# Merged input in half-length tiles, and FFN operands two blocks wide made in steps between the quarters of the projection

## The chip, the cores and the metric

The kernel runs on one core of one Trainium2 chip. The metric is the device time of one execution in microseconds (us), from which medians over executions are taken. The core's engines are TensorE (PE, with its weight loads as PEld), VectorE (DVE), ScalarE (ACT), GpSimd (POOL) and SyncE (SP, which here only issues transfers).

## The reference, cut to what matters

It is one layer of an encoder on 64 sample tokens and 1024 prompt tokens (T = 1088) of width 1024: token mixing in two branches, a gated merge, an output projection with a residual add, and a SwiGLU feed-forward network (FFN) with a hidden width of 2816, then a last norm. The part from the merge on is, in the notation of the reference:

```
m  = gate_a * (ya @ w_a) + gate_b * (yb @ w_b)          # merge
x1 = x + g1 * (m @ w_out)                               # output projection, residual
u  = rmsnorm(x1, norm2_g) * (1 + scale2) + shift2       # FFN input
h  = silu(u @ w_ff_gate) * (u @ w_ff_up)                # 1024 -> 2816
y  = rmsnorm(x1 + g2 * (h @ w_ff_down), final_g)        # 2816 -> 1024
```

Everything is float32. Before and after the change each float32 product is made of three matmuls: an operand is split into a high part (a cast to a format of fewer bits, "hi") and the remainder ("lo", a subtraction), and hi·hi, hi·lo and lo·hi are added up.

## The kernel before, in words

Activations lie transposed, 128 channels on the partitions and tokens along the free dimension, in eight channel blocks (KB = 8). The tokens are worked in two halves of HT = 544, each of two quarters of QT = 272. The stages that matter here follow each other as below; the times of the stages are in the next section.

**Merge** (L978 to L994). `mh` and `ml` are the merged input, split, in 16 tiles of all 1088 tokens in the pool `mp`.

**Output projection.** `wo_half(m, h, ws)` (L1051) makes channel block m of token half h by two calls of `wo_quarter`; each quarter is 24 matmuls (8 input blocks by 3), an add of the residual on DVE (L1040) and a square on ACT (L1046, tile `sq`). POOL adds the squares of m up to 5 into `acc`. The weights of the first half are split on POOL (`w_unit`: L52 makes hi, L58 lo), as are those of the second half, which are loaded again.

**Norm of a half.** `rstd_rows(h, sqs)` (L1077) adds the squares over the channels by matmuls against a column of ones (`ps_ss`, L1087: three sources, `acc` and the last two `sq`, for six token cuts, so 18), turns them into 1/sqrt on DVE and ACT (`v` L1090 and L1093, `rs` and `r` L82 to L87), spreads the result over the partitions by six matmuls (`ps_rr`, L1099) and copies it (L1102).

**FFN operands.** Gate and up are a Strassen-Winograd product of seven partial products, in the order 1, 6, 5, 7, 2, 3, 4. For a token half h the operand of product p is `ops[h, p]`, tiles `b{p}h` and `b{p}l`. `modulate2(h, j, r)` makes those of 1, 6, 5 and 7 from the pair of channel blocks j and j + 4: a multiplication by the norm (L1119, 128x1088), the modulation on ACT (L1123), three differences of 128x272 (L1128, L1129, L1132), an update (L1134) and four splits. `modulate2_rest(h, j)` splits those of 2, 3 and 4. For h = 0, modulate2 is called after every second m of the second half of the projection, and modulate2_rest after the last; for h = 1 both are called once after each of the first four jobs below. In all there are four calls of each for a half.

**Gate and up** (L1235 to L1306). The list `jobs` goes over the 22 blocks of 128 hidden channels: the first NF = 8 for the first token half alone, then 14 blocks for both halves, then the first 8 for the second half ("single" jobs at both ends, "double" ones between). `gate_up(i, h, ws, after)` is seven groups of 12 matmuls, one for each p, into four PSUM banks (`ps_ga` to `ps_gd`), with the partial sums evacuated after each group (`p1`, `u2`, L1242 to L1257). The weight tiles of the next job, `w{p}`, are made while a job runs its last half, by `weight_op`: `load_pair` (L1186) loads `wr_g` and `wr_u` of 512 KB each (pool tag `wr`, three buffers), POOL makes the sums S (L1203, L1204, L1210, L1215), ACT casts the hi part (L46), and DVE subtracts for the lo part (L55). The result h goes to `h_d` in device memory (L1258).

**Down** (from L1268). Six slices of hidden blocks, [0-3], [4-7], [8-11], [12-15], [16-19] and [20, 21]. `load_h` reads h back into `hr`, and splits it into `hh` and `hl`. The first slice is called after gate and up, its loads, casts and subtractions cut by token chunks. The matmuls go to `ps_fd` (L75 to L77).

The code order of a stage isn't the order on an engine: a scheduler in the build places the instructions by its own estimate of their times, within the order of dependences and the pools. What it made of the change is shown further down.

## Time and profile before

| | us |
|---|---|
| three runs | 1871.06, 1872.92, 1867.96 |
| median | 1871.06 |
| the profiled execution | 1872.33 |
| its span, first to last instruction | 1870.6 |
| PE busy in it | 1773.6 |

The profiled execution took 1.73 us more than its span, and 1.27 us more than the median. Times within the trace count from the span's start. The stages: merge until about 959, first half of the projection 959 to 1022, second half until 1078, the change to gate and up until 1095, gate and up from there until 1581, down until about 1824, and the last norm.

A row of a table of windows gives the stretch, then busy us and instructions of PE, PEld, DVE, ACT and POOL, the granted clock of TensorE as a share of full speed, the share of DMA, and GB/s. A row of the timeline gives start, duration, engine, line, operation, output and inputs, shape and count, and in brackets the idle time of the engine before it with what ended that. Durations are from start to end; instructions on DVE overlap a little at their ends, so that the pitch, from start to start, is shorter than the duration.

### The profile page before, as it was taken

To read this page: it belongs to the slowest core of one execution; us is meant where nothing else is said; L and a number is where in the kernel's file an instruction comes from. 1 tells how busy PE (TensorE), PEld (TensorE's weight loads), DVE (VectorE), ACT (ScalarE), POOL (GpSimd) and SP (SyncE) were. 2 spreads that over 40 slices of the span, in tenths; PEclk is the share of its full clock that TensorE was granted. 3 is DMA by queue.
4 is the path that set the end of the run, shared out by engine and by line. 5 is a ranking of instruction groups with operands and counts; after the bars stand their busy time and mean duration, and the time that the engine had idled before them with its cause. 6 is when DMAs were issued, how large, how long until landed. Compare 5 with 4: busy or idle time off the path is not lost. (4 is left out here: it accounts for less than half of the span.)

```text
span 1870.6 us, 31649 instructions
## 1 busy us (share of the span) xinstructions
PE 1773.6 (95%) x12412; PEld 1701.1 (91%) x12412; DVE 997.7 (53%) x1885; ACT 658.5 (35%) x1406; POOL 809.8 (43%) x661
## 2 busy tenths in 40 slices
PE   6899999999899999978989969999999998999997
PEld 4799999999888888868989969999999998999997
DVE  6623424242367576876351888644455466454435
ACT  4423424342244444444222464432333344010006
POOL 2433435352423222396575635433223356254334
PEclk9999999999999999989999979999999999999998
DMA  9433433324855564874665324332222243363102
GB/s 272 102 87 92 109 94 98 106 84 138 181 140 127 136 156 128 186 226 134 203 190 169 99 61 125 93 95 74 76 70 77 91 140 117 115 222 117 46 12 96
DMA packets 273991, 228.27 MB, mean 122 GB/s; under 512 B 11830, under 2 KB 253234, under 8 KB 273842
## 3 DMA queue, kind: packets, MB, share of 16 engines
...
q14 instruction: 51, 0.42, 0.1%
...
## 5 line engine op out<-in xcount | busy, mean ns | idle before, releaser
L76 PE MATMUL ps_fd<-hl,wh_fd 128*128 128x384 f32 (+1 forms) x480 | 157.7, 329 | 4.1 <-DVE hl L55 4.1
L77 PE MATMUL ps_fd<-hh,wl_fd 128*128 128x384 f32 (+1 forms) x480 | 156.9, 328 | 0.0
L75 PE MATMUL ps_fd<-hh,wh_fd 128*128 128x384 f32 (+1 forms) x480 | 155.2, 328 | 0.0
L55 DVE TENSOR_TENSOR w<-S,w 128x512 fp32r<-128x512 f32 x120 | 91.6, 778 | 54.5 <-ACT w L46 53.1
L46 ACT CAST w<-S 128x512 fp32r<-128x512 f32 x120 | 72.5, 621 | 115.0 <-POOL S L1204 38.7
L1215 POOL TENSOR_TENSOR S<-wr_g,S 128x512 f32<-128x512 f32 x30 | 48.0, 1599 | 149.8 <-DVE w L55 149.1
L363 DVE TENSOR_TENSOR_SCAN re<-re 128x128 f32<-128x128 f32 (+3 forms) x64 | 104.4, 1634 | 14.9 <-ACT re L359 14.4
L1321 DVE SCALAR_TENSOR_TENSOR x1f<-ps_fd,mod,x1f 128x384 f32<-128x384 f32 (+2 forms) x128 | 60.2, 496 | 97.6 <-PE ps_fd L77 97.5
L76 PEld LDWEIGHTS ps_fd<-hl,wh_fd 128*128 128x128 f32 x480 | 90.5, 188 | 5.6 <-DVE hl L55 5.6
L77 PEld LDWEIGHTS ps_fd<-hh,wl_fd 128*128 128x128 f32 x480 | 90.5, 189 | 0.0
L75 PEld LDWEIGHTS ps_fd<-hh,wh_fd 128*128 128x128 f32 x480 | 90.1, 189 | 0.4 <-issue 0.2
L46 ACT CAST hh<-hr 128x1088 fp32r<-128x1088 f32 (+2 forms) x30 | 24.0, 856 | 173.5 <-PE ps_fd L76 123.6
L1264 PE MATMUL ps_gb<-b6h,w 128*128 128x272 f32 x352 | 76.0, 294 | 5.6 <-ACT w L46 4.7
L1264 PE MATMUL ps_gc<-b3h,w 128*128 128x272 f32 x352 | 75.5, 294 | 3.0 <-DVE hst L1244 2.5
L359 ACT ACTIVATE re<-z 128x512 f32<-128x512 f32 (+2 forms) x96 | 47.3, 494 | 83.3 <-DVE z L355 68.8
L1264 PE MATMUL ps_ga<-b1h,w 128*128 128x272 f32 x352 | 75.1, 293 | 0.0
L1264 PE MATMUL ps_gd<-b4h,w 128*128 128x272 f32 x352 | 73.6, 289 | 1.2 <-DVE hst L1246 1.2
L1264 PE MATMUL ps_gc<-b5h,w 128*128 128x272 f32 x352 | 74.3, 290 | 0.0
L1264 PE MATMUL ps_ga<-b2h,w 128*128 128x272 f32 x352 | 73.9, 290 | 0.0
L1264 PE MATMUL ps_gd<-b7h,w 128*128 128x272 f32 x352 | 73.8, 289 | 0.0
L52 POOL TENSOR_SCALAR wh_fd<-wr_fd 128x1024 fp32r<-128x1024 f32 x20 | 23.1, 1157 | 114.9 <-PE ps_fd L76 101.2
L1254 POOL TENSOR_TENSOR hst<-g,hst 128x272 f32<-128x272 f32 x44 | 36.4, 827 | 84.1 <-ACT g L1253 84.1
(544 smaller groups left out, 6242.3 us busy)
## 6 DMA issues: line engine op xcount, KB each, us to landing
...
```

The lines of the kernel that those rows point to most:

```text
L46: nc.scalar.copy(out, in_)
L52: nc.gpsimd.tensor_scalar(out, in_, 1.0, 0.0, ALU.mult, ALU.add)
L55: nc.vector.tensor_sub(out, in_, h.bitcast(F32))
L75: nc.tensor.matmul(ps, wh, xh, start=first, stop=False)
L76: nc.tensor.matmul(ps, wh, xl, start=False, stop=False)
L77: nc.tensor.matmul(ps, wl, xh, start=False, stop=last)
L359: nc.scalar.activation(rest[:, c0 : c0 + w], ps, AF.Sigmoid, scale=-scale)
L363: nc.vector.tensor_tensor_scan(r, r, r, 1.0, ALU.mult, ALU.bypass)
L1215: nc.gpsimd.tensor_sub(src, a12, S[2])
L1254: nc.gpsimd.tensor_mul(h1, t["g1"], h1)
L1264: nc.tensor.matmul(ps, w[:, a, j, :], b[:, j, :], start=p in (1, 6, 5, 7) and j == 0 and k == 0, stop=j == 3 and k == 2, skip_group_check= ...
L1321: nc.vector.scalar_tensor_tensor(x1[m][:, lo:hi], ps[:, lo - s : hi - s], mod[:, 40 + m, g : g + 1], x1[m][:, lo:hi], ALU.mult, ALU.add)
```

## The change

- `mh`, `ml` become half-length tiles, 32 of 544 tokens in `mp`; the gate inputs of the merge move to a pool of their own (`gtp`). `mp` stays open until the end of gate and up, and its tiles hold further operands then: those of p = 2, 3, 4 for h = 0, the first five for h = 1, and later raw h.
- `x1t[h, jp, i]` holds two channel blocks side by side, so that `modulate2(h, jp, r)` works on two at once: differences and splits of 128x544 in place of 128x272, two calls for a half in place of four. It is a generator with a yield after each step, and covers the splits of 2, 3 and 4 as well. For h = 0 one step is taken after each quarter of the second half of the projection (rstd_rows is the chain's first); for h = 1 a step is taken in the first ten jobs after p = 1, 5 and 2.
- POOL adds the squares of m = 6 too, so that `ps_ss` is 12 matmuls in place of 18. For h = 1 they and `ps_rr` use banks of gate and up.
- The second half's weights get their hi part from ACT in place of POOL; lo stays on POOL.
- NF becomes 10. The down slices become [10-13], [14-17], [18-21], [0-3], [4-7], [8, 9], and `early_h` reads and splits the first of them in half tiles while the last ten jobs of gate and up run. The second slice is read at the start of down.
- Buffers: `sq2` 4 in place of 5, `fp5` has 10 tiles for h and 6 for raw h, and even slices take `up` tiles.

The core of the diff (unchanged and repeated lines left out):

```diff
-    mp = m1.enter_context(tc.tile_pool(name="mp", bufs=16, reuse_waits="tile"))
-    mh = [mp.tile([P, T], F32R, tag="m", name=f"mh{b}") for b in range(KB)]
-    ml = [mp.tile([P, T], F32R, tag="m", name=f"ml{b}") for b in range(KB)]
+    mp = m1.enter_context(tc.tile_pool(name="mp", bufs=32, reuse_waits="tile"))
...
+    def mtile(name, dtype=F32R):
+        return mp.tile([P, HT], dtype, tag="m", name=name)
...
+    mh, ml = [[[mtile(f"m{x}{b}_{h}") for h in range(2)] for b in range(KB)] for x in "hl"]
...
-            hi_act(mh[m][:, s:e], gts[0])
-            lo_dve(ml[m][:, s:e], gts[0], mh[m][:, s:e])
+            for lo, hi in ([(s, HT), (HT, e)] if s < HT < e else [(s, e)]):
+                h = lo // HT
+                src, r = gts[0][:, lo - s : hi - s], slice(lo - HT * h, hi - HT * h)
+                hi_act(mh[m][h][:, r], src)
+                lo_dve(ml[m][h][:, r], src, mh[m][h][:, r])
...
+                x1t[h, jp, i] = up.tile([P, T], F32, tag="u", name=f"x1_{h}_{jp}_{i}").rearrange("p (j t) -> p j t", j=2)
...
+        return x1t[h, m % 4 // 2, m // 4][:, m % 2, s - HT * h : e - HT * h]
...
-        if m < KB - 2:
+        if m < KB - 1:
             nc.gpsimd.tensor_add(acc[:, s:e], acc[:, s:e], sq)
...
+    def wo_half(m, h, ws, after):
+        sq = []
+        for i in range(2):
+            sq.append(wo_quarter(m, 2 * h + i, ws))
+            if i == 1:
+                nc.sync.dma_start(x1_d[m][:, HT * h : HT * (h + 1)], x1v(m, HT * h, HT * (h + 1)))
+            after()
         return sq
...
+    def rstd_rows(h, sq, rr, new_bank):
+        pss = new_bank(f"ps_ss{h}")
...
+            xs = [acc[:, QT * (2 * h + i) : QT * (2 * h + i + 1)], sq[i]]
+            for k, x in enumerate(xs):
                 nc.tensor.matmul(pss[:L, nt * i + j : nt * i + j + 1], x[:, t0 : t0 + L], ones[:, 0:1],
-                                 start=k == 0, stop=k == len(xs[i]) - 1)
...
+        yield
         for i in range(2):
-            nc.scalar.copy(rr[:, i, :], rows_[i])
-        return rr
+            row = new_bank(f"ps_rr{h}_{i}")[:, :QT]
...
+            nc.scalar.copy(rr[:, i, :], row)
+        yield
...
-    def modulate2(h, j, r):
...
+        x = [x1t[h, jp, i] for i in range(2)]
         rr = r.rearrange("p i t -> p (i t)")
-        nc.vector.tensor_mul(x, x, rr[:, None, :].to_broadcast([P, 2, HT]))
         for i in range(2):
...
+            nc.vector.tensor_mul(x[i], x[i], rr[:, None, :].to_broadcast([P, 2, HT]))
+            for jj in range(2):
...
+            yield
+        b11, b12, b21, b22 = x[0][:, :, :QT], x[0][:, :, QT:], x[1][:, :, :QT], x[1][:, :, QT:]
+        split(h, jp, 1, b11)
+        nc.vector.tensor_sub(b11, b12, b11)
+        yield
+        t2 = npl.tile([P, HT], F32, tag="t2", name=f"t2_{h}_{jp}", bufs=1).rearrange("p (j t) -> p j t", j=2)
+        nc.vector.tensor_sub(t2, b22, b11)
+        split(h, jp, 5, b11)
+        yield
         nc.vector.tensor_sub(b11, b21, t2)
-    def modulate2_rest(h, j):
-        x = x1t[h, j]
-        for p, src in ((2, x[:, 1, :QT]), (3, x[:, 1, QT:]), (4, x[:, 0, :QT])):
-            split(h, j, p, src)
-    def op_tile(pool, tag, h, p):
-        return [pool.tile([P, T], F32R, tag=tag, name=f"b{p}{x}_{h}").rearrange("p (j t) -> p j t", j=4) for x in "hl"]
+        split(h, jp, 6, t2)
+        yield
+        nc.vector.tensor_sub(b12, b22, b12)
+        split(h, jp, 7, b12)
+        yield
+        for p, src in ((2, b21), (3, b22), (4, b11)):
+            split(h, jp, p, src)
+            yield
+    def op_tiles(h, p, wide):
+        res = []
+        for x in "hl":
+            if wide:
+                t = up.tile([P, T], F32R, tag="u", name=f"b{p}{x}_{h}").rearrange("p (i j t) -> p i j t", i=2, j=2)
+                res.append([t[:, 0], t[:, 1]])
+            else:
+                res.append([mtile(f"b{p}{x}_{h}_{i}").rearrange("p (j t) -> p j t", j=2) for i in range(2)])
+        ops[h, p] = res
+    def step(gen):
+        next(gen, None)
...
-        sqs.append(wo_half(m, 0, ws))
...
-    r = rstd_rows(0, sqs[-2:])
...
+        sqs = wo_half(m, 0, ws, lambda: None)
+    for p in order:
+        op_tiles(0, p, order.index(p) < 4)
+    rows2 = [npl.tile([P, HT], F32, tag="rr", name=f"rr{h}", bufs=1).rearrange("p (i t) -> p i t", i=2) for h in range(2)]
+    todo = chain([rstd_rows(0, sqs, rows2[0], sbank), modulate2(0, 0, rows2[0]), modulate2(0, 1, rows2[0])])
...
-            modulate2(0, m // 2, r)
...
-    for p in order[4:]:
-        ops[0, p] = op_tile(fp, "h", 0, p)
-    r = rstd_rows(1, sqs[-2:])
-    for j in range(4):
-        modulate2_rest(0, j)
...
+        raw = wp.tile([P, KB, P], F32, tag="wr", name=f"wr_wp{m}")
+        nc.sync.dma_start(raw, cols(w_out, m * P))
+        ws = [wp.tile([P, KB, P], F32R, tag=t, name=f"{t}_wp{m}") for t in ("wh", "wl")]
+        hi_act(ws[0], raw)
+        lo_pool(ws[1], raw, ws[0])
+        sqs = wo_half(m, 1, ws, lambda: step(todo))
+    for _ in todo:
+        pass
+    for p in order:
+        op_tiles(1, p, order.index(p) >= 5)
     banks.close()
...
-    NF = 8
...
+    def early_h(i):
+        hh[i], hl[i] = (up.tile([P, T], F32R, tag="u", name=f"h{x}{i}") for x in "hl")
+        for h in range(2):
+            raw = mtile(f"hr{i}_{h}", F32)
+            r = slice(HT * h, HT * (h + 1))
+            nc.sync.dma_start(raw, h_d[i][:, r])
+            hi_act(hh[i][:, r], raw)
+            lo_dve(hl[i][:, r], raw, hh[i][:, r])
+            yield
+    NF = 10
+    slices = [list(range(NF + 4 * i, NF + 4 * i + 4)) for i in range(3)] + [[0, 1, 2, 3], [4, 5, 6, 7], [8, 9]]
...
+    def gbank(name):
+        return gb.tile([P, 512], F32, tag="g", name=name, bufs=8)
+    todo = chain([rstd_rows(1, sqs, rows2[1], gbank), modulate2(1, 0, rows2[1]), modulate2(1, 1, rows2[1])])
...
+        if k == FFB:
+            todo = chain([early_h(b) for b in slices[0]])
+        def hook(p, last):
+            if last and raw:
                 nxt[p] = weight_op(nxt_i, p, raw)
+            if (k < NF and p in (1, 5, 2)) or (k >= FFB and p == 5):
+                step(todo)
...
-            gate_up(i, h, ws, prepare if h == halves[-1] else lambda p: None)
+            gate_up(i, h, ws, lambda p: hook(p, h == halves[-1]))
...
-        if k < 4:
-            modulate2(1, k, r)
-            modulate2_rest(1, k)
+        if k == NF - 1:
+            for _ in todo:
+                pass
+    for _ in todo:
+        pass
     gst.close()
-    fst.close()
+    m1.close()
...
-    def load_h(i, parts=((0, T),)):
...
-            nc.sync.dma_start(raw[:, s:e], h_d[i][:, s:e])
-        for s, e in parts:
-            hi_act(hh[i][:, s:e], raw[:, s:e])
-            lo_dve(hl[i][:, s:e], raw[:, s:e], hh[i][:, s:e])
+        return fp.tile([P, T], dtype, tag="h", name=name, bufs=10)[:, :n]
+    def load_h(i, si):
+        raw = fp.tile([P, T], F32, tag="hr", name=f"hr{i}", bufs=6)
+        hh[i], hl[i] = (hslot(T, f"h{x}{i}", F32R) if si % 2 else up.tile([P, T], F32R, tag="u", name=f"h{x}{i}") for x in "hl")
+        nc.sync.dma_start(raw, h_d[i])
+        hi_act(hh[i], raw)
+        lo_dve(hl[i], raw, hh[i])
...
-    slices = [list(range(4 * i, 4 * i + 4)) for i in range(5)] + [[20, 21]]
-    for i in slices[0]:
-        load_h(i, CHUNKS)
     for si, blocks in enumerate(slices[:-1]):
+        if si == 0:
+            for i in slices[1]:
+                load_h(i, 1)
         ffn_down(blocks, si == 0)
-        for i in slices[si + 1]:
-            load_h(i)
+        if si >= 1:
+            for i in slices[si + 1]:
+                load_h(i, si + 1)
```

What the build makes of it is shown at three places. First TensorE at the end of the projection; `ps_wo` is the projection, `ps_ss` the sum of squares, `ps_ga` the first bank of gate and up. Before:

```order
L75 MATMUL ps_wo_3_11393<-mh_9551,wh_wp_11361 128x272
L76 MATMUL ps_wo_3_11393<-ml_9559,wh_wp_11361 128x272
L77 MATMUL ps_wo_3_11393<-mh_9551,wl_wp_11362 128x272
L1087 MATMUL ps_ss_11432<-ones,acc 128x1
L1087 MATMUL ps_ss_11432<-ones,sq_2_11308 128x1
L1087 MATMUL ps_ss_11432<-ones,sq_2_11391 128x1
```

Now:

```order
L75 MATMUL ps_wo_3_11406<-mh_1_9562,wh_wp_11370 128x272
L76 MATMUL ps_wo_3_11406<-ml_1_9578,wh_wp_11370 128x272
L77 MATMUL ps_wo_3_11406<-mh_1_9562,wl_wp_11371 128x272
L1289 MATMUL ps_ga_0_11517<-b1h_10816,w_0_11483 128x272
L1289 MATMUL ps_ga_0_11517<-b1l_10817,w_0_11483 128x272
L1289 MATMUL ps_ga_0_11517<-b1h_10816,w_0_11483 128x272 x2
```

The first twelve matmuls of gate and up stand between the projection and the sum of squares, where before the sum of squares and then `ps_rr` came first.

Second, VectorE at the same place, from the evacuation of the last quarters of the projection on; names with b are operands, `w` the split weights, `v` the sums of squares. Before:

```order
L1040 SCALAR_TENSOR_TENSOR x_1_3_10096<-ps_wo_2_11365,mod,x_1_3_10096 128x272
L1040 SCALAR_TENSOR_TENSOR x_1_3_10096<-ps_wo_3_11393,mod,x_1_3_10096 128x272
L55 TENSOR_TENSOR b2l_11427<-x_0_0_10089,b2h_11426 128x272
L55 TENSOR_TENSOR b2l_11427<-x_0_1_10090,b2h_11426 128x272
L55 TENSOR_TENSOR b2l_11427<-x_0_2_10091,b2h_11426 128x272
L55 TENSOR_TENSOR b2l_11427<-x_0_3_10092,b2h_11426 128x272
L55 TENSOR_TENSOR b3l_11429<-x_0_0_10089,b3h_11428 128x272
L55 TENSOR_TENSOR b3l_11429<-x_0_1_10090,b3h_11428 128x272
L55 TENSOR_TENSOR b3l_11429<-x_0_2_10091,b3h_11428 128x272
L55 TENSOR_TENSOR b3l_11429<-x_0_3_10092,b3h_11428 128x272
L55 TENSOR_TENSOR b4l_11431<-x_0_0_10089,b4h_11430 128x272
L1090 TENSOR_SCALAR v_11433<-ps_ss_11432 128x2
```

Now:

```order
L1051 SCALAR_TENSOR_TENSOR x_1_1_1_10132<-ps_wo_2_11374,mod,x_1_1_1_10132 128x272
L1051 SCALAR_TENSOR_TENSOR x_1_1_1_10132<-ps_wo_3_11406,mod,x_1_1_1_10132 128x272
L55 TENSOR_TENSOR w_0_11493<-S_0_11486,w_0_11493 128x512
L55 TENSOR_TENSOR w_0_11506<-S_0_11504,w_0_11506 128x512
L55 TENSOR_TENSOR w_1_11535<-wr_g_11512,w_1_11535 128x512
L1105 TENSOR_SCALAR v_11539<-ps_ss_11538 128x2
L1108 TENSOR_SCALAR v_11539<-ps_ss_11538 16x1
L1105 TENSOR_SCALAR v_11539<-ps_ss_11538 128x2
L1108 TENSOR_SCALAR v_11539<-ps_ss_11538 16x1
L55 TENSOR_TENSOR w_0_11509<-wr_u_11481,w_0_11509 128x512
L83 RECIPROCAL r_11557<-rs_11558 128x6
L84 TENSOR_TENSOR rs_11558<-r_11557 128x6
```

The splits of operands 2, 3 and 4 for h = 0 (b2l, b3l, b4l), which followed the last evacuation, have gone ahead of it, and splits of the weights stand in their place. From there to the evacuation `u` of the fourth job (block 3) there are 116 rows before and 79 now. All steps for h = 1 stand in that stretch, so among the first three jobs, though the code spreads them over ten.

Third, the transfers that SP issues around the first single jobs of the second half; `wr_g` and `wr_u` are the raw weights, `hr` raw h, and the store is that of h. Before:

```order
L1186 DMA wr_g_16258<-in_w_ff_gate 128x8x128
L1186 DMA wr_u_16260<-in_w_ff_up 128x8x128
L1258 DMA h_d<-hst_1_16125 128x544
L1186 DMA wr_g_16395<-in_w_ff_gate 128x8x128
L1309 DMA hr_17193<-h_d 128x384 x2
L1186 DMA wr_u_16397<-in_w_ff_up 128x8x128
L1258 DMA h_d<-hst_1_16262 128x544
L1186 DMA wr_g_16532<-in_w_ff_gate 128x8x128
L1309 DMA hr_17205<-h_d 128x384 x2
L1186 DMA wr_u_16534<-in_w_ff_up 128x8x128
```

Now:

```order
L1211 DMA wr_g_15861<-in_w_ff_gate 128x8x128
L1302 DMA hr_0_15926<-h_d 128x544
L1302 DMA hr_1_16067<-h_d 128x544
L1302 DMA hr_0_16210<-h_d 128x544
L1302 DMA hr_1_16351<-h_d 128x544
L1302 DMA hr_0_16494<-h_d 128x544
L1302 DMA hr_1_16635<-h_d 128x544
L1302 DMA hr_0_16778<-h_d 128x544
L1302 DMA hr_1_16919<-h_d 128x544
L1283 DMA h_d<-hst_0_15620 128x544
L1211 DMA wr_u_15863<-in_w_ff_up 128x8x128
```

The eight loads of the first down slice stand in one block behind the first single job's `wr_g`, ahead of a store and of that job's `wr_u`. Before, they went in pairs, one to a job.

More of the change, by code (lines that the diff above doesn't have):

```diff
@@ L1000, in trunk @@
     for h in range(2):
-        for j in range(4):
-            x1t[h, j] = up.tile([P, T], F32, tag="u", name=f"x1_{h}_{j}").rearrange("p (i t) -> p i t", i=2)
+        for jp in range(2):
+            for i in range(2):
+                x1t[h, jp, i] = up.tile([P, T], F32, tag="u", name=f"x1_{h}_{jp}_{i}").rearrange("p (j t) -> p j t", j=2)
     acc = npl.tile([P, T], F32, tag="acc", name="acc", bufs=1)
@@ L1034, in wo_quarter @@
         (wh, wl), s, e = ws, QT * q, QT * (q + 1)
+        h, r = q // 2, slice(QT * (q % 2), QT * (q % 2 + 1))
         ps = dbank(f"ps_wo{m}_{q}")
         for kb in range(KB):
-            mm3(ps[:, :QT], wh[:, kb, :], wl[:, kb, :], mh[kb][:, s:e], ml[kb][:, s:e], kb == 0, kb == KB - 1)
+            mm3(ps[:, :QT], wh[:, kb, :], wl[:, kb, :], mh[kb][h][:, r], ml[kb][h][:, r], kb == 0, kb == KB - 1)
         for lo, hi, g in by_group(s, e):
@@ L1075, in rstd @@
         return r
-    def rstd_rows(h, sqs):
-        pss = dbank(f"ps_ss{h}")
+    def rstd_rows(h, sq, rr, new_bank):
+        pss = new_bank(f"ps_ss{h}")
         nt = -(-QT // P)
@@ L1082, in rstd_rows @@
         nc.vector.memset(v, 1.0)
-        xs = [[acc[:, QT * (2 * h + i) : QT * (2 * h + i + 1)]] + [sq[i] for sq in sqs] for i in range(2)]
         cuts = [(i, j, P * j, min(P, QT - P * j)) for i in range(2) for j in range(nt)]
         for i, j, t0, L in cuts:
-            for k, x in enumerate(xs[i]):
+            xs = [acc[:, QT * (2 * h + i) : QT * (2 * h + i + 1)], sq[i]]
+            for k, x in enumerate(xs):
                 nc.tensor.matmul(pss[:L, nt * i + j : nt * i + j + 1], x[:, t0 : t0 + L], ones[:, 0:1],
-                                 start=k == 0, stop=k == len(xs[i]) - 1)
+                                 start=k == 0, stop=k == len(xs) - 1)
         for i in range(2):
@@ L1095, in rstd_rows @@
         rsqrt_cols(npl, r, v, 2 * nt, "6")
-        rr = npl.tile([P, HT], F32, tag="rr", name=f"rr{h}", bufs=1).rearrange("p (i t) -> p i t", i=2)
-        rows_ = [sbank(f"ps_rr{h}_{i}")[:, :QT] for i in range(2)]
-        for i, j, t0, L in cuts:
-            nc.tensor.matmul(rows_[i][:, t0 : t0 + L], r[:L, nt * i + j : nt * i + j + 1].to_broadcast([L, P]), ident[:L, :L],
-                             start=True, stop=True)
-        for i in range(2):
-            nc.scalar.copy(rr[:, i, :], rows_[i])
@@ L1103, in rstd_rows, with split @@
-        return rr
+        yield
+        for i in range(2):
+            row = new_bank(f"ps_rr{h}_{i}")[:, :QT]
+            for i_, j, t0, L in cuts:
+                if i_ == i:
+                    nc.tensor.matmul(row[:, t0 : t0 + L], r[:L, nt * i + j : nt * i + j + 1].to_broadcast([L, P]), ident[:L, :L],
+                                     start=True, stop=True)
+            nc.scalar.copy(rr[:, i, :], row)
+        yield
     ops = {}
-    def split(h, j, p, src):
+    def split(h, jp, p, src):
@@ L1263, in gate_up @@
                 for k, (a, b) in enumerate(((0, oh), (0, ol), (1, oh))):
-                    nc.tensor.matmul(ps, w[:, a, j, :], b[:, j, :], start=p in (1, 6, 5, 7) and j == 0 and k == 0,
+                    nc.tensor.matmul(ps, w[:, a, j, :], b[j // 2][:, j % 2, :], start=p in (1, 6, 5, 7) and j == 0 and k == 0,
                                      stop=j == 3 and k == 2, skip_group_check=True)
```

63 lines of the change are left out of this document (17 added, 46 removed).

## The prediction

> **What bounds the kernel now.** I read the page first, for the engine that sets the pace.
>
> ```profile
> PE 1773.6 (95%) x12412; PEld 1701.1 (91%) x12412; DVE 997.7 (53%) x1885; ACT 658.5 (35%) x1406; POOL 809.8 (43%) x661
> ```
>
> TensorE is busy for 95% of the span, so the change can only gain where PE isn't at full pace: it waits, or runs at a lower clock. The windows say where, for the stages that are edited.
>
> ```profile
> core 0: us, PE busy (x) PEld busy (x) DVE busy (x) ACT busy (x) POOL busy (x), PEclk, DMA share, GB/s
> 1025.00:1032.00 7.00, 7.00 (x39) 6.97 (x38) 1.71 (x11) 0.64 (x2) 0.54 (x1) 0.52 0.27 75
> 1032.00:1078.00 46.00, 46.00 (x368) 45.70 (x367) 40.90 (x49) 20.89 (x48) 33.12 (x23) 1.00 0.32 101
> 1184.00:1294.00 110.00, 109.53 (x863) 108.30 (x862) 56.43 (x106) 36.32 (x74) 39.64 (x35) 1.00 0.29 86
> 1404.00:1493.00 89.00, 89.00 (x711) 89.00 (x710) 43.70 (x83) 28.88 (x57) 27.62 (x26) 1.00 0.27 82
> 1493.00:1581.00 88.00, 85.36 (x654) 82.46 (x652) 55.50 (x96) 35.45 (x74) 47.16 (x38) 1.00 0.45 131
> 1581.00:1590.00 9.00, 4.92 (x18) 3.89 (x19) 8.90 (x6) 3.80 (x10) 9.00 (x5) 0.81 0.35 117
> 1590.00:1824.00 234.00, 234.00 (x1422) 233.51 (x1421) 108.96 (x186) 19.16 (x18) 93.59 (x47) 1.00 0.30 102
> 1077.94:1145.14 67.20, 51.51 (x360) 49.59 (x359) 58.43 (x119) 40.54 (x92) 25.86 (x17) 0.82 0.25 73
> ```
>
> The double jobs (1404 to 1493) and down (1590 to 1824) run without a gap: 89 / 711 = 0.1252 us for a gate-up matmul, 10.5 us for a gate_up of 84, and 234 / 1422 = 0.165 us in down. Nothing is to be had there. Time is lost in four places: at half clock just after 1025, in the change from the projection to gate and up, in the last single jobs, and at the start of down. The timeline and the waits take the second apart.
>
> ```profile
> 1077.94 0.29 PE L77 MATMUL ps_wo<-mh,wl_wp 128*128 128x272 f32 x1
> 1083.24 0.15 DVE L1090 TENSOR_SCALAR v<-ps_ss 128x2 f32<-128x2 f32 x1
> 1089.45 0.69 DVE L55 TENSOR_TENSOR w<-S,w 128x512 fp32r<-128x512 f32 x1 [1.71 <-ACT w L46]
> 1090.66 1.13 DVE L87 TENSOR_TENSOR r<-r,rs 128x6 f32<-128x6 f32 x1
> 1091.93 3.42 PE L1099 MATMUL ps_rr<-ident,r 128*128 128x128 f32 x12 [8.75 <-DVE r L87]
> 1095.28 0.59 PE L1264 MATMUL ps_ga<-b1h,w 128*128 128x272 f32 x1
> 1095.80 4.90 DVE L1119 TENSOR_TENSOR x<-x,rr 128x1088 f32<-128x1088 f32 x4 [4.02 <-ACT rr L1102]
> 1145.14 0.42 DVE L1242 TENSOR_TENSOR u<-ps_gb,p 128x272 f32<-128x272 f32 x1
> 1215.99 0.29 PE L1264 MATMUL ps_ga<-b1h,w 128*128 128x272 f32 x1
> ```
>
> Call the last projection matmul t0 = 1077.94. The first gate matmul starts at 1095.28, 17.34 us later, because the build puts all of the norm's chain in front of it, and the chain's DVE steps stand behind splits of weights. From 1095.80 on DVE is the bound: it has nearly all operands of h = 1 to make while PE works three jobs. The row at 1145.14 is the fourth job's evacuation of product 6, and the last ends the tenth gate_up: 138.05 us after t0, where ten of them are 840 x 0.1252 = 105.2 us.
>
> **The change part by part.** *Second half of the projection.* Six `ps_ss` products fewer, of two passes each.
>
> ```profile
> 1022.97 0.58 PE L1087 MATMUL ps_ss<-ones,sq 128*128 128x1 f32 x4
> ```
>
> At 0.58 / 4 = 0.145 us a pass, 12 passes are 1.7 us. Behind them stands the half clock of the row 1025 to 1032, in which PE never idled: 7 us at 0.52 cost 7 x 0.48 = 3.4 us. Whether 24 passes in a block still bring it on, no row shows; so the term is 1.7 to 5.1 us, and I take 3, near the lower end, as the block is still some 3 us long. The Trainium skill ("TensorE: Matmul & The Clock Gate", Part 1, the two states) puts the lower clock down to an idle window of about 3.4 us; this row differs, since PE was busy with one-column matmuls all the time. By the page alone the term would be 1.7.
>
> ```profile
> 1079.94 1.50 DVE L55 TENSOR_TENSOR b2l<-x,b2h 128x272 fp32r<-128x272 f32 x4 [0.48 <-ACT b2h L46]
> ```
>
> The splits of operands 2, 3 and 4, which move into this stage, are three such groups, 4.5 us; with them DVE has 40.90 + 4.5 of 46 us, and the hi part of the weights goes to ACT, which is busy for 20.89 of 46. So both cost nothing; without this cover DVE would run over by a us or two.
>
> *From t0 to the tenth gate_up.* PE no longer waits for the norm, since twelve matmuls of job 0 and then more follow t0 directly. What decides is DVE. I count its instructions from t0 to the evacuation at 1145.14 in the order of both builds, and price them by pitches of uncontended rows.
>
> ```profile
> 1126.32 0.68 DVE L55 TENSOR_TENSOR w<-wr_g,w 128x512 fp32r<-128x512 f32 x1
> 1126.92 0.43 DVE L1246 TENSOR_TENSOR hst<-ps_gd,hst 128x272 f32<-128x272 f32 x1
> 1127.27 0.68 DVE L55 TENSOR_TENSOR w<-S,w 128x512 fp32r<-128x512 f32 x1
> ```
>
> 512 columns take 0.60 and 272 take 0.35; the four of 1088 above 4.90 / 4 = 1.22; 544 lies between, an estimate of 0.64. Before: 28 x 0.60 + 75 x 0.35 + 4 x 1.22 and nine tiny ones (0.07 to 0.15) make 48.9 us. After: 25 x 0.60 + 19 x 0.35 + 22 x 0.64 + 4 x 1.22 and the nine make 41.3: the splits of h = 0 are gone from the stretch, and two narrow operations cost 0.06 more than a wide one. Before, DVE was in fact busy for 58.43 us of the 67.20 (window above), 1.195 times the price. So after, 41.3 x 1.195 = 49.3, and I add 3 us of idle time in place of 8.77, as it waits for `rr` with weights to split: the evacuation comes at t0 + 52.3. By then PE has done 256 matmuls of gate and up in the order (293 before), which are 32 us, beside 24 x 0.145 = 3.5 for `ps_ss` and half of the 3.42 that `ps_rr` took at half clock: 37 us, so PE isn't the bound. Left are 840 - 256 = 584 at 0.1252, 73.1 us.
>
> To this comes the weight ring, which paces single jobs: three raw buffers, and in each round a load, three sums, a split and a fourth sum on POOL.
>
> ```profile
> 1493.12 1.73 POOL L1203 TENSOR_TENSOR S<-wr_u 128x512 f32<-128x512 f32 x1 [2.09 <-DMA wr_u<-in_w_ff_up]
> 1564.93 1.28 POOL L1203 TENSOR_TENSOR S<-wr_u 128x512 f32<-128x512 f32 x1 [2.25 <-DMA wr_u<-in_w_ff_up]
> 1532.44 0.29 PE L1264 MATMUL ps_ga<-b1h,w 128*128 128x272 f32 x1
> 1544.60 0.29 PE L1264 MATMUL ps_ga<-b1h,w 128*128 128x272 f32 x1
> 1568.24 0.29 PE L1264 MATMUL ps_ga<-b1h,w 128*128 128x272 f32 x1
> ```
>
> A round is (1564.93 - 1493.12) / 6 = 11.97 us, against 10.5 on PE. Double jobs have 21 us for it, so PE lives off a lead and then falls to the ring's pace: 12.16, and (1568.24 - 1544.60) / 2 = 11.82 us a job. At the start the same shows as 1215.99 - 1145.14 = 70.85 us for 840 - 293 = 547 matmuls, 68.5: 2.3 us lost. Two more single jobs, about 1 us each, make it 4.3. So the tenth gate_up ends at t0 + 52.3 + 73.1 + 4.3 = 129.7, which is 8.3 us earlier. The bounds: 41.3 x 1.0 + 3 wins 16 us, 41.3 x 1.35 + 3 wins 2; what lies beyond is a rival.
>
> *Last single jobs.* Before, the last four run (1580.56 - 1532.44) - 4 x 10.5 = 6.1 us over.
>
> ```profile
> 1580.56 0.77 PE L75 MATMUL ps_fd<-hh,wh_fd 128*128 128x320 f32 x2
> 1581.52 10.71 DVE L55 TENSOR_TENSOR hl<-hr,hh 128x320 fp32r<-128x320 f32 x8
> PE ps_fd L76 <- DVE hl L55: 4.1, 3, 2.9
> ```
>
> After, two more jobs at the ring's pace add 2 x 1.47 = 2.9. The eight loads of h stand on SP's queue between the first job's `wr_g` and its `wr_u`, and wait there for the raw half tiles, which are free once h = 0's operands have been read for the last time; behind them wait a store and `wr_u`, and with that POOL's sums and the first single job's groups. The casts and subtractions stand ahead of evacuations of that job on ACT and DVE. The eight loads alone take eight issues; a pair takes this:
>
> ```profile
> 1506.48 0.81 SPq L1309 DMA_DIRECT2D hr<-h_d  x2
> ```
>
> so 3.2 us, which go off the lead. I take 2.5, between nothing and 5. The loss after is 6.1 + 2.9 + 2.5 = 11.5.
>
> *Start of down.* The first slice is split by then, so the wait for `hl` goes: 9 us hold 18 matmuls, 18 x 0.165 = 3.0, so 6.0 are won. What is late next is `wl_fd` from POOL, which is 9.00 of 9.00 busy there; if it is, half of this is lost. Both together: 6.0 - (11.5 - 6.1) = +0.6, from -4 to +5.
>
> *Merge, buffers, slices.* Half tiles cut one of three chunks in two, 16 short pieces more on ACT and DVE, which wait for PE there; nothing, give or take 1.5. The later slices stand as many jobs ahead as before, under a down that is all PE; nothing.
>
> The sum is 3 + 8.3 + 0.6 = 11.9 us off the profiled execution's 1872.33, 1860.4; that execution lies 1.27 over the median, and 1871.06 - 11.9 is 1859.2. I say **1860**.
>
> **The rivals.** *PE is the bound after all.* If the wide operations leave DVE free of contention and the build's crowding of three jobs is undone by waits elsewhere, the evacuation comes at t0 + 37 and the tenth gate_up at 37 + 73.1 + 2.3 = 112.4: 25.7 us won, with the others 29.3, so **1842**. For it speaks that DVE idled 8.77 us before; against it that 41.3 us are more than 37 even without contention.
>
> *POOL shuts DVE out.* The four splits b2l, 1.50 us above, a second time:
>
> ```profile
> 1118.38 4.70 DVE L55 TENSOR_TENSOR b2l<-x,b2h 128x272 fp32r<-128x272 f32 x4
> 1120.96 1.47 POOL L1210 TENSOR_TENSOR S<-wr_g,wr_u 128x512 f32<-128x512 f32 x1
> ```
>
> The second ended when POOL's three sums did. If all of POOL's 25.86 us in the stretch stood in DVE's way and not 9.5 (58.4 - 48.9), DVE would need 41.3 + 25.9 = 67.2 and the tenth gate_up end at 144.6, 6.6 late: 3 - 6.6 + 0.6 = -3, **1874**. Against it: the measured share is 9.5 of 25.9. The Trainium skill ("SBUF — State Buffer", two separate sides) says that a DVE operation with two inputs and a GpSimd one lock each other out for a whole instruction, whichever starts first; these rows agree.
>
> *The ring gets longer: slower.* Each round waits for DVE's split, and DVE now holds wider operations and the early slice ahead of it. With a round of P us governing the 584 matmuls (6.95 jobs) after the evacuation and all ten last jobs, the gain is 3 + (138.05 - 52.3 - 6.95 P) + 6.0 + 6.1 - 10 (P - 10.5). It is nothing at P = 12.1, and over 0.3% slower from 12.5 on; at 12.8 it is -11, **1882**. For it: 11.97 is near. Against it: the lead that the double jobs build up, and that the row at 1564.93 had the old splits of the slice in it already.
>
> **How the numbers follow.** My forecast has 0.64, PE-bound 0.12, POOL 0.13, the ring 0.11. The forecast's own range is 1851 to 1868, from the terms' bounds (1.7 to 5.1, 2 to 16, -4 to 5, 1.5 either way) where they don't all fall on one side. 0.3% of 1871 is 5.6 us, about what a measurement of this kernel can tell from no change; 1865.4 is the edge. Faster: 0.92 of the forecast and PE-bound, 0.71. Slower: the ring, 0.11. Same: the rest, 0.18. The range runs from the PE-bound case to the POOL case, 1842 to 1874; it leaves out the ring and half of the first rival.
>
> **What would show it.** Right: no window at half clock around 1025; the first gate matmul at once after the last of `ps_wo`, and the evacuation of block 3 some 52 us behind it, with DVE busy throughout; last single jobs of 11.5 to 12 us; `ps_fd` at full pace from the start. Wrong: evacuation at 37 (PE-bound) or over 60 (POOL), rounds of L1203 over 12.5 us (ring), or a wait of PE for `hl` or `wl_fd` in down's first us.

## The result and the profile after

The changed kernel takes 1877.16 us (median of 9 runs, 1873.3 to 1879.83) against 1871.06 (9 runs, 1862.56 to 1873.86). The ratio is 1.0036, 95% interval 1.0021 to 1.0052: slower by 0.2 to 0.5%, where 1860 and a range up to 1874 were forecast.

The profiled execution of the changed kernel is its fastest one, 1873.30 us with a span of 1871.6. Its part ahead of the merge, which the change doesn't touch, ended 3.2 us earlier than in the profile before (902.92 against 906.12; the other profiles lie between 899.9 and 906.3). So the two profiles are compared stage by stage, from the first matmul of the merge on:

| stage, by first and last matmuls on PE | before | after | forecast | found |
|---|---|---|---|---|
| merge | 52.36 | 54.29 | 0 | +1.9 |
| first half of the projection | 63.79 | 63.35 | 0 | -0.4 |
| second half, to t0 (the last projection matmul) | 55.67 | 53.60 | -3 | -2.1 |
| t0 to the end of ten gate_ups | 138.06 | 137.98 | -8.3 | -0.1 |
| from there to 2856 gate-up matmuls (ten gate_ups before the end) | 253.20 | 255.18 | 0 | +2.0 |
| the rest of gate and up | 111.08 | 115.80 | +5.4 | +4.7 |
| to the 101st matmul of down | 23.53 | 19.80 | -6.0 | -3.7 |
| rest | 266.8 | 268.7 | 0 | +1.9 |

The sum is 4.2 us, beside 6.1 between the medians. The page of the changed kernel has PE as busy as before:

```profile
PE 1774.8 (95%) x12388; PEld 1700.0 (91%) x12388; DVE 1010.6 (54%) x1859; ACT 667.9 (36%) x1404; POOL 812.6 (43%) x665
```

Now the windows that answer to those of before (stretch, then busy us and instructions of PE, PEld, DVE, ACT, POOL, clock, DMA share, GB/s):

```profile
1025.00:1030.00 5.00, 5.00 (x32) 4.96 (x32) 1.21 (x10) 1.23 (x2) 0.00 (x0) 0.66 0.36 105
1074.16:1143.22 69.06, 55.40 (x370) 53.53 (x369) 60.50 (x85) 38.30 (x71) 30.28 (x23) 0.84 0.23 70
1493.00:1583.00 90.00, 85.53 (x637) 80.86 (x636) 56.55 (x99) 35.71 (x74) 46.76 (x38) 1.00 0.41 119
1583.00:1593.00 10.00, 7.25 (x45) 6.80 (x44) 2.56 (x6) 0.00 (x0) 8.99 (x5) 1.00 0.38 113
1593.00:1824.00 231.00, 231.00 (x1397) 231.00 (x1396) 103.38 (x174) 19.06 (x18) 92.06 (x46) 1.00 0.31 103
```

The second row is the one that matters: from t0 to the fourth job's evacuation there are 69.06 us, not the forecast 52.3, and DVE is busy for 60.50 of them. The clock in it is 0.84, before it was 0.82. The timeline of the changed kernel at the marks used before:

```profile
1074.16 0.28 PE L77 MATMUL ps_wo<-mh,wl_wp 128*128 128x272 f32 x1
1074.77 0.90 DVE L1051 SCALAR_TENSOR_TENSOR x<-ps_wo,mod,x 128x272 f32<-128x272 f32 x2
1079.46 0.56 PE L1289 MATMUL ps_ga<-b1h,w 128*128 128x272 f32 x1 [5.02 <-DVE x L1051]
1086.23 0.16 DVE L1105 TENSOR_SCALAR v<-ps_ss 128x2 f32<-128x2 f32 x1 [0.96 <-PE ps_ss L1102]
1095.86 4.90 DVE L1136 TENSOR_TENSOR x<-x,rr 128x1088 f32<-128x1088 f32 x4 [1.59 <-ACT rr L1118]
1143.22 0.43 DVE L1267 TENSOR_TENSOR u<-ps_gb,p 128x272 f32<-128x272 f32 x1
1212.14 0.29 PE L1289 MATMUL ps_ga<-b1h,w 128*128 128x272 f32 x1
```

PE starts gate and up 5.30 us after t0 in place of 17.34, and not at once behind it, as had been forecast: it waits 5.0 us for the last evacuations of the projection. These stand on DVE behind splits of weights, and end at t0 + 5.56 (before, at t0 + 1.52). From within this wait on the granted clock is at half for 13.6 us; the last row is its window.

```profile
1076.32 0.91 DVE L55 TENSOR_TENSOR w<-S,w 128x512 fp32r<-128x512 f32 x1 [0.65 <-ACT w L46]
1077.15 1.75 DVE L55 TENSOR_TENSOR w<-wr_g,w 128x512 fp32r<-128x512 f32 x1
1078.83 0.90 DVE L1051 SCALAR_TENSOR_TENSOR x<-ps_wo,mod,x 128x272 f32<-128x272 f32 x2
1076.90:1090.50 13.60, 11.04 (x55) 11.01 (x56) 9.02 (x18) 4.28 (x10) 6.79 (x5) 0.50 0.29 88
```

The multiplications by the norm come at t0 + 21.7, later than before (17.9), and all of the 12 us is gone by the tenth gate_up. What PE waits for in between:

```profile
PE ps_ga L1289 <- DVE x L1051: 5.0, 1, 5.0
PE ps_gc L1289 <- DVE hst L1269: 4.8, 2, 4.0
PE ps_gb L1289 <- ACT w L46: 1.9, 1, 1.9
PE ps_gb L1289 <- DVE w L55: 1.9, 2, 1.3
```

Most of it is for evacuations and weight splits on DVE. Four rows of DVE and POOL show what delays them:

```profile
1112.90 0.71 DVE L55 TENSOR_TENSOR b6l<-t,b6h 128x544 fp32r<-128x544 f32 x1
1121.39 1.80 DVE L55 TENSOR_TENSOR b1l<-x,b1h 128x544 fp32r<-128x544 f32 x1
1120.99 1.62 POOL L1228 TENSOR_TENSOR S<-wr_u 128x512 f32<-128x512 f32 x1 [0.70 <-DVE b2l L55]
1122.69 1.65 POOL L1229 TENSOR_TENSOR S<-S,wr_g 128x512 f32<-128x512 f32 x1
```

A wide split takes 0.71 us with POOL idle and 1.80 beside POOL's sums, and POOL's sums get longer too (1.62 and 1.65; with DVE idle one takes 1.29, as in a row of e2 below). The Trainium skill ("SBUF — State Buffer", two separate sides) says that a VectorE operation with two inputs in SBUF and a GpSimd one that reads SBUF shut each other out; these rows agree.

### The profile page after: what moved, and what is told of

Read it like the earlier page. It is cut to its first block, busy times and chain, and to the rows that moved or that the text cites. A ratio compares the mean times of both kernels' runs of the same rounds, so it can differ in the third digit from the quotient of the medians.

```text
span 1871.6 us, 31615 instructions
## 1 busy us (share of the span) xinstructions
PE 1774.8 (95%) x12388; PEld 1700.0 (91%) x12388; DVE 1010.6 (54%) x1859; ACT 667.9 (36%) x1404; POOL 812.6 (43%) x665
## 5 line engine op out<-in xcount | busy, mean ns | idle before, releaser
L55 DVE TENSOR_TENSOR w<-S,w 128x512 fp32r<-128x512 f32 x128 | 104.8, 833 | 61.5 <-ACT w L46 59.9
L46 ACT CAST w<-S 128x512 fp32r<-128x512 f32 x128 | 76.8, 619 | 134.4 <-POOL S L1229 44.3
L46 ACT CAST hh<-hr 128x1088 fp32r<-128x1088 f32 (+1 forms) x26 | 24.0, 961 | 177.5 <-PE ps_fd L76 148.0
L1228 POOL TENSOR_TENSOR S<-wr_u 128x512 f32<-128x512 f32 x32 | 42.4, 1325 | 83.8 <-DMA wr_u<-in_w_ff_up 74.8
```

The costliest lines, as they stand in the source:

```text
L46: nc.scalar.copy(out, in_)
L55: nc.vector.tensor_sub(out, in_, h.bitcast(F32))
L1228: nc.gpsimd.tensor_add(S[1], a21, a22)
```

## The experiments

All numbers of the start below count from t0 to the end of the tenth gate_up (840 gate-up matmuls); those of the last jobs are what their ten gate_ups lose against 10.54 us each. The expectations speak of theory A (the work for h = 1 crowds DVE) and theory B (the weight ring paces the start); A2, A3 and A4 are told where they come up.

| run | time, us (ratio to before, interval) | tenth gate_up | last jobs lose |
|---|---|---|---|
| before | 1871.06 | 138.06 | 5.7 |
| changed kernel | 1877.16 (1.0021 to 1.0052) | 137.98 | 10.5 |
| e1_late | 1881.59 (1.0032 to 1.0071) | 139.46 | 12.0 |
| e2_repack | 1883.81 (1.0049 to 1.0093) | 139.93 | 20.5 |
| e3_nf8 | 1872.56 (0.9989 to 1.0018) | 136.13 | 7.1 |
| e4_noh1, less work | 1854.52, one run | 121.98 | 9.2 |
| e5_sums | 1862.02 (0.9925 to 0.9958) | 141.71 | 0.0 |
| e6_nf8_sums | 1863.17 (0.9925 to 0.9964) | 139.54 | 0.1 |
| e8_spread | 1878.06 (1.0016 to 1.0052) | 138.77 | 9.1 |
| e9_spread_tail | 1865.88 (0.9961 to 0.9986) | 139.67 | 1.3 |
| e10_nf8_spread_tail | 1860.68 (0.9929 to 0.9960) | 139.48 | 0.0 |
| e11_nf8_tail | 1860.75 (0.9930 to 0.9962) | 136.24 | 0.0 |
| e12_nosums, less work | 1855.55, one run | 115.53 | 10.5 |
| e13_dummy, other work | 1861.22, one run | 127.97 | 10.5 |
| e14_before_tail | 1864.45 (0.9941 to 0.9974) | 138.36 | 0.0 |

**Is it the crowding in the first three jobs?** Holding the steps for h = 1 back, in e1_late until the banks of the third job are free:

```diff
-            if (k < NF and p in (1, 5, 2)) or (k >= FFB and p == 5):
+            if (k == 0 and p == 1) or (3 <= k < NF and p in (1, 5, 2)) or (k >= FFB and p == 5):
```

> The sum of squares for h = 1 is made in job 0 as before, the other steps for h = 1 only from the fourth job on (their rows' PSUM banks come free after job 2), so that they don't stand among the first three jobs. Theory A (crowding on VectorE: the steps for h = 1 hold up splits of weights and evacuations): the tenth gate_up ends at t0 + 126 to 131 in place of 138.0, the time falls by 5 to 10 us. Theory B (the weight ring alone paces the start, whatever VectorE does beside it): 136 to 140, time within 2 us of the changed kernel.

The first job still loses 12.9 us (5.3 of them before its first matmul, with half clock behind), the second and third run at PE's pace, and the work costs 18 us in the next three; 139.46 in all. Theory A, read as "it stands in the wrong jobs", falls, and so far B stands. One row shows the stretching again: the four multiplications that took 4.90 us.

```profile
1120.95 8.16 DVE L1136 TENSOR_TENSOR x<-x,rr 128x1088 f32<-128x1088 f32 x4
```

**Can the weight ring be shortened by another packing?**

```diff
-        for w, nm in ((w_g, "g"), (w_u, "u")):
+        for x, nm in enumerate("tb"):
...
+            for y, w in enumerate((w_g, w_u)):
+                nc.sync.dma_start(raw[:, 4 * y : 4 * y + 4], cols(w, i * P)[:, 4 * x : 4 * x + 4])
```

> The raw weights of a job are packed otherwise: one buffer holds the first halves of gate's and up's block (read for the last time at p = 7), the other the second halves (p = 2, 3, 4); same bytes, four loads of half the size. The ring's round should get shorter, since the first buffer comes free three groups of 12 matmuls earlier (3 x 1.5 = 4.5 us less of waiting). Theory B: the start ends at 126 to 132 and the last single jobs lose 2 to 5 us in place of 10.4, together 10 us faster or more. Theory A: the last single jobs lose 2 to 5 us, the start gains 3 us at most, so 5 to 9 us faster.

It was slower, and neither theory's number came. The build put POOL's sum for p = 7, the last reader of the first buffer, at the end of the round, so the buffer came free later. The ring's round, from one first sum to the next, is (1556.28 - 1496.72) / 5 = 11.9 us in the changed kernel:

```profile
1496.72 1.29 POOL L1228 TENSOR_TENSOR S<-wr_u 128x512 f32<-128x512 f32 x1 [2.93 <-DVE hst L1271]
...
1556.28 1.29 POOL L1228 TENSOR_TENSOR S<-wr_u 128x512 f32<-128x512 f32 x1 [3.21 <-DMA wr_u<-in_w_ff_up]
```

Here, in e2:

```profile
1509.69 1.29 POOL L1229 TENSOR_TENSOR S<-wr_t,wr_b 128x512 f32<-128x512 f32 x1 [8.99 <-DMA wr_b<-in_w_ff_up]
1522.32 1.28 POOL L1229 TENSOR_TENSOR S<-wr_t,wr_b 128x512 f32<-128x512 f32 x1 [5.84 <-DMA wr_b<-in_w_ff_up]
1535.31 1.30 POOL L1229 TENSOR_TENSOR S<-wr_t,wr_b 128x512 f32<-128x512 f32 x1 [6.18 <-DMA wr_b<-in_w_ff_up]
```

That is 12.8 us ((1535.31 - 1509.69) / 2), and the last jobs lose 20.5 in place of 10.5. As a test of the start it failed; for the last jobs it shows that they follow the ring's round.

**What do two more single jobs cost?**

```diff
-    NF = 10
-    slices = ... + [[0, 1, 2, 3], [4, 5, 6, 7], [8, 9]]
+    NF = 8
+    slices = ... + [[0, 1, 2, 3], [4, 5, 6, 7], [20, 21]]
```

> NF back to 8, with the slices of down moved accordingly ([8-11], [12-15], [16-19], [0-3], [4-7], [20, 21]); everything else as changed. If two more single jobs at the ring's pace cost what was summed up: 1.8 us less at the start (after the tenth gate_up) and 2.5 to 3 less in the last jobs, 4 to 5 us faster. If single and double jobs cost the same, within 1 us.

4.6 us less than the changed kernel (1872.56), as summed up, though each execution varies by as much. In the profiles it is 3.6 us by the eleventh gate_up (146.70 against 150.31) and 3.4 in the last jobs, less 3 us in other stages.

**What does the work for h = 1 cost?**

```diff
-    todo = chain([rstd_rows(1, sqs, rows2[1], gbank), modulate2(1, 0, rows2[1]), modulate2(1, 1, rows2[1])])
+    todo = chain([])
...
-        op_tiles(1, p, order.index(p) >= 5)
+        ops[1, p] = ops[0, p]
```

> Leaves out the operands of h = 1 altogether (norm, modulation, differences and splits; the second token half multiplies the operands of h = 0). Theory A: without 19 us of VectorE work the tenth gate_up ends at t0 + 115 to 122. Theory B: it still ends after t0 + 132. The last jobs and the start of down stay as in the changed kernel, within 2 us.

The tenth gate_up ends at 121.98, 16 us earlier, the upper edge of theory A; theory B, which put it after 132, falls. Without that work DVE has time to spare:

```profile
1085.00:1130.00 45.00, 45.00 (x359) 45.00 (x359) 27.43 (x49) 20.28 (x40) 23.06 (x19) 1.00 0.32 94
```

27.43 of 45 us busy, so 17.6 free in four jobs. 8.1 us are lost by 336 matmuls, all of them in the first job (the wait of 5.3 us at its start, and half clock). From the fifth job on the ring shows here too: 16.5 by 840.

**Sums on VectorE.** In e5 for the single jobs at both ends, in e6 with NF = 8:

```diff
+        eng = nc.vector if i < NF else nc.gpsimd
...
-            nc.gpsimd.tensor_add(S[1], a21, a22)
-            nc.gpsimd.tensor_sub(S[2], S[1], a11)
+            eng.tensor_add(S[1], a21, a22)
+            eng.tensor_sub(S[2], S[1], a11)
```

and likewise for the other two sums.

> The four weight sums of the jobs with i < NF (the single jobs, at both ends) go from POOL to VectorE, where one of 512 columns has a pitch of 0.60 us: 2.4 us more VectorE work for each single job, and almost no POOL work beside it. Theory A2 (what the wider operations should win is lost because VectorE and POOL hold each other up: 58.8 us busy for a price of 41.3): the tenth gate_up ends at t0 + 122 to 131 in place of 138.0, and the ring's round falls below PE's 10.5 us, so that the last jobs lose 1 to 5 us in place of 10.4; time 12 to 20 us below the changed kernel. Rival (VectorE is simply full, and contention is a small part): the tenth gate_up at 140 to 148, the last jobs 1 to 5, time within 5 us of the changed kernel.

> The same with NF = 8 and its slices of down. Theory A2: beats both kernels, 1852 to 1860. If the ring no longer paces single jobs, NF should matter no more: within 2 us of the run with NF = 10. Rival: 1868 to 1876.

Both are faster than both kernels, by times that lie within theory A2 for the first and between the two theories for the second. In the last jobs the loss is gone altogether: with a sum at 0.69 us in place of 1.29 the ring's round drops below PE's pace. NF no longer matters (1862.02 and 1863.17). At the start it went as the rival said: 141.71. DVE is busy for most of the time still, now with sums (the first 68.27 us after t0):

```profile
1075.33:1143.60 68.27, 58.70 (x377) 56.43 (x375) 57.92 (x102) 38.22 (x71) 5.45 (x6) 0.83 0.24 72
```

The clock is 0.83 here, with PE busy for 58.70 us, so part of this start's loss may be the clock's; no run separates the two.

**Is the merge's loss due to the cut pieces?** In e7 the kernel before, with the middle chunk's hi and lo in two pieces:

```diff
-            hi_act(mh[m][:, s:e], gts[0])
-            lo_dve(ml[m][:, s:e], gts[0], mh[m][:, s:e])
+            for lo, hi in ([(s, HT), (HT, e)] if s < HT < e else [(s, e)]):
+                hi_act(mh[m][:, lo:hi], gts[0][:, lo - s : hi - s])
+                lo_dve(ml[m][:, lo:hi], gts[0][:, lo - s : hi - s], mh[m][:, lo:hi])
```

> The kernel before with one part of the change alone: hi and lo of the middle chunk of the merge are made in two pieces (320 to 544, 544 to 704), into the same tiles of 1088. The changed kernel's merge, from its first matmul to the first transpose of the projection, took 54.3 us against 52.4. If the cut pieces are the reason, 53.7 to 54.5 here; if it is the pools of half tiles, 52.4 give or take 0.4.

The merge took 55.4 us (904.23 to 959.62), against 52.4 before and 54.3 in the changed kernel: the pieces are enough to explain it, though it is one execution; its time was 1877.29. The other profiles agree: with the pieces the merge takes 52.9 to 55.4 us in all 14 kernels, without them 52.4 and 52.6 (before and e14).

**Does it help to hold the work back in two portions?** Each pair gets its own spread of the norm, bound to banks of the third and of the sixth job:

```diff
+    def second():
+        rr = npl.tile([P, HT], F32, tag="rr", name="rr1b", bufs=1).rearrange("p (i t) -> p i t", i=2)
+        yield from spread_rows(1, rr, gbank)
+        yield from modulate2(1, 1, rr)
...
+            if (k == 0 and p == 1) or (2 <= k < 5 and p in (1, 5, 2)) or (k == 5 and p == 1) or (6 <= k < NF and p in (1, 5, 2)) or (k >= FFB and p == 5):
```

> The operands of h = 1 for the first pair of blocks are held back until the banks of the third job come free, those of the second pair until the sixth job (the norm's rows are spread a second time for them, 6 matmuls and 2 copies more), so that VectorE gets half of the work at a time. The run without the work left VectorE free for 17.6 of 45 us in the first jobs. Theory A3 (what costs is that the build packs the work of h = 1 into some three jobs, more than VectorE has free there): the tenth gate_up ends at t0 + 122 to 130 in place of 138.0, time 6 to 14 us below the changed kernel. Rival (the work costs the same wherever it stands, since the single jobs' ring needs VectorE all the time): 136 to 141, time within 3 us.

> The same, and the weight sums of the jobs after the double ones on VectorE, those of the start on POOL. The last jobs lose nothing (10.4 us less than the changed kernel, as in the run with all single jobs' sums there), and nothing changes at the start against the run before. Theory A3: 17 to 24 us below the changed kernel, 1853 to 1860. Rival: 8 to 12 below, 1865 to 1869.

> The same with NF = 8, the pairs held back until the second and the fifth job. Theory A3 with the ring's 1.1 us for each further single job at the start: 2 us less than with NF = 10 if two pairs still fit, up to 4 us more if they crowd.

> NF = 8 with the last jobs' sums on VectorE and the work of h = 1 as the build packs it. From the run with NF = 8 (6.9 us lost in the last jobs, none here): 6 to 8 us below it, 1864 to 1868. Theory A3: 4 to 12 us slower than the same with the work held back; rival: within 2 us of it.

The tail's edit in the last three is `eng = nc.vector if late_job[0] else nc.gpsimd`, set from the last double job on. A3 falls: 138.77, each pair costing some 10 us. The times are the rival's too: e9 is 11.3 us below the changed kernel, and e11, 3 us better than expected, is level with e10. NF = 8 without holding back has the earlier tenth gate_up (136.24 against 139.48). The last jobs' loss goes as in e5; a sum on VectorE in e11, and PE in its last jobs (stretch, PE busy and so on):

```profile
1503.75 0.69 DVE L1229 TENSOR_TENSOR S<-wr_u 128x512 f32<-128x512 f32 x1 [0.61 <-DMA wr_u<-in_w_ff_up]
```

```profile
1492.00:1573.00 81.00, 81.00 (x647) 81.00 (x646) 67.88 (x124) 34.58 (x71) 11.53 (x12) 1.00 0.43 129
```

In e8 one wait of PE shows how a portion costs what DVE as a whole would have time for; the DVE rows up to its end:

```profile
PE ps_gc L1297 <- DVE hst L1277: 5.3, 2, 5.0
```

```profile
1128.08 1.46 DVE L55 TENSOR_TENSOR b6l<-t,b6h 128x544 fp32r<-128x544 f32 x1
1129.46 1.78 DVE L1159 TENSOR_TENSOR x<-x,t 128x544 f32<-128x544 f32 x1
1131.17 1.78 DVE L55 TENSOR_TENSOR b7l<-x,b7h 128x544 fp32r<-128x544 f32 x1
1132.87 0.71 DVE L55 TENSOR_TENSOR b2l<-x,b2h 128x544 fp32r<-128x544 f32 x1
1133.51 0.43 DVE L1277 TENSOR_TENSOR hst<-ps_gc,u 128x272 f32<-128x272 f32 x1
```

The order on an engine is fixed by the build. It puts four steps for a later token half ahead of an evacuation that PE needs now; three of them are stretched from 0.71 to 1.5 to 1.8 us while POOL sums.

**POOL's part, split in two.** e12 leaves out the sums of the first single jobs (the products take raw blocks); e13 adds as many sums that nobody reads:

```diff
+        if i < NF and not last_jobs[0]:
+            src = {1: a11, 6: a22, 5: a21, 7: a11, 2: a12, 3: a12, 4: a22}[p]
```

```diff
+            for n in range({6: 2, 7: 1, 3: 1}.get(p, 0)):
+                nc.gpsimd.tensor_add(new("S1"), w[:, 0].bitcast(F32), w[:, 0].bitcast(F32))
```

> Leaves out the weight sums of the first single jobs (their products take the raw blocks), so that at the start POOL neither stands in the ring's round nor works beside VectorE; VectorE's own work is unchanged. Theory A4 (what the wider operations should have won is lost to POOL, through the ring's round or by stretching VectorE's operations): the tenth gate_up ends at t0 + 118 to 128 in place of 138.0. Rival (VectorE's own work for h = 1 and the weights is the bound): 132 to 139.

> The same, but POOL makes four sums of the same size for each of these jobs that nobody reads, from the split weights: it works beside VectorE as before, and isn't in the ring's round. If it is the stretching of VectorE's operations, 132 to 139, as in the changed kernel; if it is the ring's round, within 3 us of the run without the sums.

115.53 and 127.97 against 137.98. The first is below the range of A4, the second is neither of its two numbers but between them. So POOL's sums cost 22.4 us at the start: 12.4 by working beside DVE (127.97 - 115.53), and 10.0 by standing in the chain from load to split, with what follows from that (137.98 - 127.97). These are single executions. The second share isn't the ring's pace alone, as a table of what is lost against 10.54 us a job shows:

| us lost by the end of | job 1 | job 4 | job 10 |
|---|---|---|---|
| changed kernel | 14.5 | 28.1 | 32.6 |
| e13, sums that nobody reads | 7.1 | 16.1 | 22.6 |
| e12, no sums | 5.1 | 8.4 | 10.1 |

Of the 10.0 us between the first two rows 7.4 are there after one job. In e13 the splits of the weights aren't late, PE waits 1.34 us at the start in place of 5.02, and the clock doesn't fall (1.00 in the window below, 0.84 in the changed kernel):

```profile
1072.12 0.36 PE L1294 MATMUL ps_ga<-b1h,w 128*128 128x272 f32 x1 [1.34 <-DVE x L1051]
```

How much of the 10.0 is the half clock isn't shown; no run has the sums in the chain and the full clock. From t0 to the fourth job's evacuation, e12 and then e13:

```profile
1078.98:1130.15 51.17, 49.01 (x380) 47.14 (x379) 45.99 (x85) 36.24 (x67) 7.28 (x4) 1.00 0.30 89
```

```profile
1070.50:1130.46 59.96, 51.80 (x389) 48.63 (x388) 57.63 (x85) 36.49 (x67) 30.45 (x22) 1.00 0.25 76
```

The same 85 DVE instructions are busy for 45.99 us beside 7.28 us of POOL, and for 57.63 beside 30.45: 11.6 us more DVE time for 23.2 us of POOL. Both windows are at full clock, so this difference is not the clock's. (The build orders the two a little differently, so a microsecond or two of either share may belong to the other; and the sums of e13 read the split weights, which they may hold longer.) One difference, L1148, in both:

```profile
1118.71 0.71 DVE L1148 TENSOR_TENSOR t<-x,x 128x544 f32<-128x544 f32 x1
```

```profile
1116.15 1.56 DVE L1148 TENSOR_TENSOR t<-x,x 128x544 f32<-128x544 f32 x1
```

**What of the change is worth keeping?** The tail's edit alone, on the kernel before:

> The kernel before with one edit: the sums of the last single jobs on VectorE, as in the run with NF = 8 and this edit (1860.7). The last jobs lost 5.8 us before and should lose nothing: 1864 to 1867. What is left between this and 1860.7 is what the change brings without its two further single jobs (the start of down, the second half of the projection, less the merge): 3 to 6 us.

1864.45, as expected. The change with NF = 8 and the same edit is at 1860.75, 3.7 us lower, but beside runs of the kernel before with other medians (1872.46 and 1870.84); by the ratios it is 2 us, and their intervals overlap. So what the rest of the change brings isn't clear of the noise.

## Why the prediction was wrong

- **The step that failed** is the 52.3 us from t0 to the evacuation of block 3: "Before, DVE was in fact busy for 58.43 us of the 67.20 (window above), 1.195 times the price. So after, 41.3 x 1.195 = 49.3, and I add 3 us of idle time". It took 69.06, 16.8 more. DVE came to the first of the counted instructions at t0 + 5.56, not at t0, since splits of weights and the projection's last evacuations stood in front of them. The counted work then took 55.60 us and not 49.3, and DVE idled for 7.9 and not 3:

```profile
1079.73:1143.22 63.49, 54.85 (x367) 53.17 (x367) 55.60 (x78) 36.19 (x67) 25.38 (x18) 0.85 0.24 72
```

- Why the ratio failed: the prices were near, but what comes on top of them isn't a property of DVE's work. All 85 instructions between the two marks come to some 44.5 us by the prediction's pitches; e12, with 7.28 us of POOL left, has them busy for 45.99 and the evacuation at 51.17. The rest is what POOL does beside them: some 16 us for its 30.28 in the changed kernel; before, priced the same way, 8.5 for 25.86. (The terms given for the 41.3 add up to 41.6 with the same nine tiny ones; that changes nothing.)
- That the tenth gate_up came only 8.3 us later than forecast (137.98 against 129.7), and not 16.8, is luck. Counted by the build's order, 256 gate-up matmuls were to be done by the evacuation; on the chip it was 331 (the 370 of the window less 24 `ps_ss`, 12 `ps_rr` and 3 `ps_wo`), which is 9.4 us more. Of the rest, 5.2 us were lost and not 4.3.
- The rival "POOL shuts DVE out" (0.13) gave an evacuation over 60 as its sign, and that came. Its mechanism is worth 12.4 us (e13 against e12), and its time of 1874 was still below the measured 1877.16.
- What the sums cost by standing in the chain, 10.0 us, the prediction had only as the ring's pace from the fourth job on. It had PE start "directly" behind t0; most of the 10.0 falls into the first job, with the wait of 5.02 us and the half clock behind it, which the sum didn't have either.
- After the tenth gate_up, 2.0 us were lost that the sum left out: the ring's pace reaches into the eleventh gate_up (150.31 - 137.98 = 12.3 us). e3 and e11, with NF = 8, don't have it (10.6).
- The last jobs were right in kind and size, 4.7 us against 5.4; with NF = 8 (e3) 3.4 of them are gone. The eight loads in one block, which I gave 2.5 us, aren't seen as a cost by themselves: with the sums on DVE, e5 and e11 have them too and lose nothing.
- The start of down was right in kind, 3.7 in place of 6.0. The prediction said that half of the gain is lost if `wl_fd` is late, and it was; 0.6 us went to an evacuation:

```profile
1584.03 0.38 PE L75 MATMUL ps_fd<-hh,wh_fd 128*128 128x320 f32 x1 [0.62 <-DVE hst L1281]
1586.68 0.42 PE L77 MATMUL ps_fd<-hh,wl_fd 128*128 128x320 f32 x1 [2.12 <-POOL wl_fd L58]
```

- The second half gained 2.1 of 3; the half clock came again, for a shorter time. In e5 and e8, where it didn't come, the stage took 52.1 us in place of 53.6. The merge lost 1.9 where 0 was taken: cut pieces cost (e7).
- Down's matmuls are slower by 1.65 us over the last 1339 of 1440, a little everywhere and with PE never idle (221.91 against 220.26), in every run built on the changed kernel alike. Why stays open.
